# Two transformer blocks on one core: the left factors of the down products are formed beside gate and up and kept in DRAM

## The chip, the cores and the metric

One Trainium2 chip, and one of its cores. The engines of a core are TensorE (PE, the matmuls), VectorE (DVE), ScalarE (ACT), GpSimd (POOL) and SyncE (SP, which here only issues transfers). The metric is the device time of one execution in microseconds (us).

## The reference

Two transformer blocks, one behind the other, on 1024 tokens of width 1024, all in fp32. Each block ends in a feed-forward network (FFN) of hidden width 2816, and the change lies in these two:

```python
gu = jnp.einsum('bsd,df->bsf', x, w_gu)                      # block 1
gate, up = gu[..., :FFN_HIDDEN], gu[..., FFN_HIDDEN:]
ffn = jnp.einsum('bsf,fd->bsd', jax.nn.silu(gate) * up, w_down)
...
h = rmsnorm(x, g_ffn_pre[l]) * (1.0 + scale_f) + shift_f     # block 2
f = (jax.nn.silu(h @ w_gate[l]) * (h @ w_up[l])) @ w_down[l]
x = x + gate_f * rmsnorm(f, g_ffn_post[l])
```

Ahead of the first FFN stand three mixers and an output projection; ahead of the second, stick-breaking attention, a pooling mixer and another output projection. The change does not touch how these compute.

## The kernel before, in words

**Numbers.** A matmul of fp32 quality is made of three: each factor is split into a high half (a cast on ACT, line L80 or L938) and a low half (the remainder, a subtraction on DVE or POOL, L84 or L939), and `mm3` (L95 to L99) multiplies high by high, high by low and low by high.

**Gate and up** (`gate_up`, L1000 to L1058). The hidden width is 22 tiles of 128, taken as 11 pairs. The tiles of pairs 0 and 1 are multiplied directly (`direct`, tiles f = 0 to 3). Pairs 2 to 10 each go through two `Matrix` objects, `Gate` and `Up` (L899 on): seven products each, in the order 1, 6, 2, 7, 5, 4, 3, of the weights (or sums of two quarters of them, the `tt` tiles) with quarters of the activations, kept ready in SBUF as split tiles `x1B11`, `x1T2` and so on (in the second network `x3...`). `product` (L932) takes a tile `wst` from the ring of slots "w", splits the weights into it (ACT and then DVE or POOL) and issues 12 matmuls; `after` adds the sum to those of earlier products (tiles `p`, `u`, `s`). `Up.out` multiplies the silu of the gate by up (DVE for the first quarter, POOL L987 for the other three) and queues a store of the 128x512 result to `h_d` in DRAM, which ACT issues (L1056).

**Down** (`down`, L1077 on). Groups of 1, 2, 2, 2 and 2 pairs, seven products for each group. The rows of h are loaded back (`hr`) beside the weights (`wr`); sums S1 to S4 and T1 to T4 are formed (`st`), both factors are split (`hs` into slots "w", `ws` into a pool of its own). The last four tiles go directly (`down_last`, L1168) and are split there (`last`).

**What sets the order.** Each engine runs its instructions in one order, which a list scheduler writes at build time; `soon()` raises the priority of what is inside it. A tile from a ring waits for the last reader of the tile that had the slot before. The ring "w" has 6 slots and "raw" has 3. SP issues the loads, and ACT the stores of h.

Of the kernel before, what the change touches and what calls it, by code (L numbers as in the profile page):

```python
# [38 lines left out]
def two_blocks(ctx: ExitStack, tc: tile.TileContext, a):  # L39
# [657 lines left out]
    def out_proj(wo, mix_t, into, norm, put, ahead):  # L697


        mt = {0: mix_t(0)}  # L700
        for tb in range(NB + ahead):
            if tb + 1 < NB:
                mt[tb + 1] = mix_t(tb + 1)
            if tb >= ahead:
                put(tb - ahead)
            if tb < NB:
                out_block(wo, mt.pop(tb), tb, into)
                norm(tb)
# [32 lines left out]
    x1p, x1_done = pool("x1p")  # L741

    class Act:


        def __init__(self, pl, name):
            self.pl, self.name, self.t = pl, name, {}

        def half(self, th):
            if th not in self.t:  # L750
                self.t[th] = [self.pl.tile([P, KT, 512], F32R, tag="act", bufs=4, name=f"{self.name}{th}{p}")
                              for p in "hl"]
            return self.t[th]
# [25 lines left out]
    class SAct:  # L779
# [4 lines left out]
        def __init__(self, pl, name):  # L784
            self.pl, self.name, self.t = pl, name, {}

        def __call__(self, n):
            if n not in self.t:
                if n in ("T2", "T3"):

                    new = lambda nm: accp.tile([P, 4, 512], F32R, tag="acc", bufs=4, name=nm)
                else:
                    new = lambda nm: self.pl.tile([P, 4, 512], F32R, tag="act", bufs=10, name=nm)
                self.t[n] = [new(f"{self.name}{n}{p}") for p in "hl"]
            return self.t[n]
# [4 lines left out]
        def temp(self):  # L800
            return self.pl.tile([P, 4, P], F32, tag="tt", bufs=4, name="tt")
# [78 lines left out]
    x1 = SAct(x1p, "x1")  # L880
# [6 lines left out]
    out_proj(wo, lambda tb: turned(tb, 512), add1, norm1, lambda tb: x1.put(acc[tb], tb), 2)  # L887
    wo_done.close()

    x2_d = dr.tile([S, D], F32, name="x2_d")
    x3_d = dr.tile([S, D], F32, name="x3_d")
    mod_d = dr.tile([6, D], F32, name="mod_d")

    h_d = [dr.tile([P, S], F32, name=f"h_d{f}") for f in range(NFT)]
# [83 lines left out]
    class Up(Matrix):  # L981
        def out(self, i, l, t, o):
# [5 lines left out]
            self.stores.append((h_d[self.f + i][:, l * 512:(l + 1) * 512], s))  # L988

    def gate_up(act, wg, wu, nraw, npost, extra=None):  # L990

        gp, gp_done = pool("gp")
        n_raw = [0]

        def wide():
            return gp.tile([P, KT, P], F32, tag="rw", bufs=nraw, name="rw")

        def load(src):
            n_raw[0] += 1
            if nraw < 4 and n_raw[0] % 5 >= nraw:  # L1000
                r = slot("raw", [P, KT, P], F32, "raw")
            else:
                r = wide()
            DMA.dma_start(r, src)
            return r

        def post(nm):
            return gp.tile([P, 512], F32, tag="post", bufs=npost, name=nm)

        def own(tag, shape, dtype, name):  # L1010
            return gp.tile(shape, dtype, tag="rw", bufs=nraw, name=name) if tag == "w" else slot(tag, shape, dtype, name)

        def direct(f, th, g, u):
            pg = ps_lg()
            for n, (wh, wl) in enumerate((g, u)):
                for k in range(KT):
                    mm3(pg[:, n, :], wh[:, k, :], wl[:, k, :], act.at(0, k, th), act.at(1, k, th), k == 0, k == KT - 1)
            s = post("silu")
            with soon():
                A.activation(s, pg[:, 0, :], AF.Silu)  # L1020
                V.tensor_tensor(s, s, pg[:, 1, :], op=OP.mult)
            DMA.dma_start(h_d[f][:, th * 512:(th + 1) * 512], s)

        def load_gu(f, alloc=slot):
            return load_split(wg(f), [P, KT, P]), load_split(wu(f), [P, KT, P], alloc=alloc)

        wt = [load_gu(0), load_gu(1, own)]
        for th in range(2):
            for f in range(2):
                direct(f, th, *wt[f])  # L1030
        for f in (2, 3):
            wt = load_gu(f)
            for th in range(2):
                direct(f, th, *wt)
        act.sums()
        stores = []

        def flush():
            for dst, src in stores:
                A.dma_start(dst, src)  # L1040
            stores.clear()

        for p in range(2, NFT // 2):
            f = 2 * p
            ms = {}
            for m in range(2):
                w = (wg, wu)[m]
                ms[m] = (Gate, Up)[m]([load(w(f)), load(w(f + 1))], act, post)
                if m == 1:
                    ms[1].gate, ms[1].f, ms[1].stores = ms[0], f, stores  # L1050
                for q in (1, 6, 2, 7, 5, 4, 3):
                    old = list(stores)
                    stores.clear()
                    ms[m].product(q)
                    for dst, src in old:
                        A.dma_start(dst, src)  # L1056
                    if extra is not None:
                        extra(wide)  # L1058
        flush()
        gp_done.close()  # L1060

    DP = {"rw": (2 * D, 6), "st": (2 * 512, 6), "c": (2 * 512, 6), "ac": (4 * 512, 3)}

    class DownPool:


        def __init__(self, name, order):
            self.st = ExitStack()
            self.pl = {}
            for tag in order:  # L1070
                self.pl[tag], done = pool(f"{name}_{tag}")
                self.st.push(done)

        def tile(self, shape, dtype, tag, name):
            return self.pl[tag].tile(shape, dtype, tag=tag, bufs=DP[tag][1], name=name)

    def down(dp, wd, sizes, nlast, res=None):  # L1077
# [3 lines left out]
        ys = [accp.tile([P, 2, D], F32, tag="acc", bufs=4, name="acc") for _ in range(NB // 2)]  # L1081
        y = [ys[i // 2][:, i % 2, :] for i in range(NB)]
        own = {p: dp.tile([P, 4, 512], F32, "ac", f"dacc{p}") for p in (1, 6, 5)}

        def acc_of(p, c0, n):


            if p in own:
                return own[p][:, c0:c0 + n, :]
            t = ys[c0 // 2 + (0 if p in (2, 3) else 2)]  # L1090
            return t[:, c0 % 2:c0 % 2 + n, slice(0, 512) if p in (2, 4) else slice(512, D)]

        def load2(srcs, nm, small=False):
            if small:
                t = slot("raw", [P, 1, D], F32, nm)
            else:
                t = dp.tile([P, 2, D], F32, "rw", nm)
            for j, src in enumerate(srcs):
                DMA.dma_start(t[:, j, :], src)
# [601 lines left out]
```

## Time and profile before

| | us |
|---|---|
| time before, median of 3 runs | 2610.46 (2607.62 to 2612.67) |
| profiled execution, its own time | 2614.44 |
| profiled execution, its span | 2612.7 |
| PE busy | 2385.6 (91%) |
| DVE busy | 1791.0 (69%) |
| ACT busy | 1083.4 (41%) |
| POOL busy | 1031.4 (39%) |

The profiled execution lies 4.0 us above the median and has 1.7 us outside its span. By the trace, the first FFN runs from about 655 to 1400 us (direct tiles to 766, pairs from there, down from 1140, last tiles from 1340 to 1400) and the second from about 1870 to the end (pairs from 2000, down from 2360, last tiles from 2548).

### The profile page before, as it was taken

The numbers are of one execution on the slowest core, as the hardware profiler recorded it, in microseconds if no ns is written. First come the engines' busy times: TensorE is split into PE (matmuls) and PEld (weight loads), VectorE is DVE, ScalarE is ACT, GpSimd is POOL, SyncE is SP. The second block draws the span as 40 slices with busy tenths as digits, with TensorE's granted clock in tenths as the row PEclk, the third lists the DMA queues.
The fourth block names the chain that finished last, engine by engine and source line by source line (L and its number), as shares of the span: only waits on it lengthen the run. The fifth ranks groups of instructions, "written<-read, shape, count | busy, mean of one in ns | idle before, by whom it ended". The sixth has DMA issues, their size and how long they took to land.

```text
span 2612.7 us, 32305 instructions
## 1 busy us (share of the span) xinstructions
PE 2385.6 (91%) x11584; PEld 1962.2 (75%) x11584; DVE 1791.0 (69%) x2772; ACT 1083.4 (41%) x1893; POOL 1031.4 (39%) x831
## 2 busy tenths in 40 slices
PE   8888897999699999989998989889879999998997
PEld 8877776787577777867867868677657888876885
DVE  3889969646756777669976365676673555548995
ACT  4658884343223233333336334545642223225332
POOL 2520235116712222256655042435671223227646
PEclk9998998999899999989998999999989999999998
DMA  5144455423253455262304434562511222214313
GB/s 183 61 137 128 122 165 165 113 77 111 90 184 125 158 170 159 79 249 87 136 15 145 147 84 135 157 175 79 198 65 50 84 81 83 79 61 169 129 65 113
DMA packets 149787, 314.31 MB, mean 120 GB/s; under 512 B 19574, under 2 KB 65654, under 8 KB 149628
## 3 DMA queue, kind: packets, MB, share of 16 engines
q1 hardware_dynamic: 139260, 293.38, 35.4%
q10 hardware_dynamic: 10368, 18.88, 1.9%
q8 instruction: 91, 1.49, 0.2%
q14 instruction: 68, 0.56, 0.1%
HBM read 230.39 MB, written 81.81 MB: 119 GB/s over the span
## 4 chain that ended last, share of the span: by engine, by line
PE 40%; DVE 4%; POOL 3%; issue 3%; ACT 2%; DMA 2%; SPq 0%; DVEq 0%; ACTq 0%; POOLq 0%
PE plg L97 5%; PE plg L98 5%; PE plg L99 5%; PE pmm L97 5%; PE pmm L98 5%; PE pmm L99 5%; PE ptr L98 1%; PE ptr L99 1%; PE ptr L97 1%; PE plg L337 1%; POOL last L84 1%; DVE sab L1503 1%; PE ptr L1525 1%; PE pmm L692 1%; PE pmm L693 1%
## 5 line engine op out<-in xcount | busy, mean ns | idle before, releaser
L938 ACT CAST wst<-tt 128x512 fp32r<-128x512 f32 x144 | 89.3, 621 | 250.3 <-PE plg L99 202.8
L939 POOL TENSOR_TENSOR wst<-rw,wst 128x512 fp32r<-128x512 f32 x51 | 74.9, 1469 | 264.2 <-ACT wst L938 94.4
L84 POOL TENSOR_TENSOR wl<-raw,wh 128x1024 fp32r<-128x1024 f32 (+2 forms) x28 | 65.9, 2359 | 227.4 <-ACT wh L80 201.2
L337 PE MATMUL plg<-qk,qk 128*128 128x384 f32 (+4 forms) x480 | 126.1, 379 | 27.1 <-DVE mn L350 14.7
L97 PE MATMUL plg<-ws,hs 128*128 128x512 f32 x288 | 115.4, 401 | 5.2 <-DVE acc L1154 2.5
L98 PE MATMUL plg<-ws,hs 128*128 128x512 f32 x288 | 114.7, 398 | 0.0
L1503 DVE TENSOR_TENSOR_SCAN sab<-sab 128x640 f32<-128x640 f32 (+7 forms) x64 | 101.2, 1586 | 19.5 <-ACT sab L1501 18.9
L99 PE MATMUL plg<-ws,hs 128*128 128x512 f32 x288 | 114.5, 398 | 0.0
L278 ACT ACTIVATE junk_a<-xi,cand 128x1024 bf16<-128x1024 f32 (+1 forms) x124 | 109.2, 880 | 12.0 <-DVE cand L267 6.9
L337 PEld LDWEIGHTS plg<-qk,qk 128*128 128x128 f32 x480 | 82.4, 199 | 37.9 <-DVE mn L350 16.4
L939 DVE TENSOR_TENSOR wst<-tt,wst 128x512 fp32r<-128x512 f32 x144 | 105.9, 737 | 6.9 <-ACT wst L938 6.3
L84 POOL TENSOR_TENSOR hs<-hr,hs 128x1024 fp32r<-128x1024 f32 (+1 forms) x30 | 71.3, 2377 | 83.5 <-ACT hs L80 69.7
L1212 DVE SCALAR_TENSOR_TENSOR mod<-raw_c,sc,mod 128x1024 f32<-128x1024 f32 x42 | 55.9, 1331 | 57.3 <-DMA raw_c<-in_w_cond_dram 57.3
L162 PE MATMUL pmm<-wh,xh 128*128 128x256 f32 (+1 forms) x320 | 92.3, 289 | 1.6 <-DVE stgl L399 0.8
L938 ACT CAST wst<-rw 128x512 fp32r<-128x512 f32 x77 | 47.6, 619 | 108.4 <-PE plg L99 56.6
L987 POOL TENSOR_TENSOR u<-u,u 128x512 f32<-128x512 f32 x36 | 56.0, 1556 | 91.2 <-issue 43.5
L163 PE MATMUL pmm<-wl,xh 128*128 128x256 f32 (+1 forms) x320 | 91.5, 286 | 0.0
L164 PE MATMUL pmm<-wh,xl 128*128 128x256 f32 (+1 forms) x320 | 91.5, 286 | 0.0
L961 DVE TENSOR_TENSOR u<-plg,u 128x512 f32<-128x512 f32 x36 | 24.9, 690 | 96.5 <-PE plg L99 96.5
L351 ACT ACTIVATE e<-e,mn 128x128 f32<-128x128 f32 (+7 forms) x96 | 74.3, 774 | 36.1 <-DVE mn L350 35.3
L80 ACT CAST wh<-raw 128x1024 fp32r<-128x1024 f32 x54 | 56.5, 1050 | 73.2 <-PE pmm L98 30.8
L97 PE MATMUL pmm<-xh,wh 128*128 128x512 f32 x192 | 79.3, 413 | 7.4 <-DVE oB L585 4.8
(563 smaller groups left out, 8419.2 us busy)
## 6 DMA issues: line engine op xcount, KB each, us to landing
raw_c<-in_w_cond_dram SPq DMA_DIRECT2D x48, 512.0 KB, 4.1
hr<-h_d SPq DMA_DIRECT2D x44, 512.0 KB, 4.4
wr<-in_w_down_dram SPq DMA_DIRECT2D x44, 512.0 KB, 4.3
qk<-qkd SPq DMA_DIRECT2D x72, 256.0 KB, 5.7
rw<-in_wgu_dram SPq DMA_DIRECT2D x36, 512.0 KB, 4.3
x_d<-acc SPq DMA_DIRECT2D x24, 512.0 KB, 2.9
qk<-qk2d SPq DMA_DIRECT2D x48, 256.0 KB, 4.5
raw<-in_wqk_dram SPq DMA_DIRECT2D x20, 512.0 KB, 5.4
```

What stands on the lines that cost most here:

```text
L84: eng.tensor_tensor(lo, src, hi.bitcast(F32), op=OP.subtract)
L97: T.matmul(out, lh, rh, start=start, stop=False, skip_group_check=more)
L98: T.matmul(out, lh, rl, start=False, stop=False, skip_group_check=more)
L99: T.matmul(out, ll, rh, start=False, stop=stop, skip_group_check=more)
L162: T.matmul(o, at(0, k, tb * P, P), h[:, j, :], start=(k == 0), stop=False)
L163: T.matmul(o, at(0, k, tb * P, P), l[:, j, :], start=False, stop=False)
L164: T.matmul(o, at(1, k, tb * P, P), h[:, j, :], start=False, stop=(k == KT - 1))
L278: A.activation(junk_a[:, :L], xi[self.blks[i]], AF.Sign, bias=c, accum_out=self.cnt[:, i:i + 1])
L337: T.matmul(pl[:, c, :n], q[:, isl], k2[:, c * n:(c + 1) * n], start=(j == 0), stop=last)
L938: A.copy(wh, x)
L939: (G if p in (2, 4) else V).tensor_tensor(wl, x, wh.bitcast(F32), op=OP.subtract)
L1503: V.tensor_tensor_scan(sa[:, ::-1], sa[:, ::-1], sa[:, ::-1], 1.0, op0=OP.mult, op1=OP.bypass)
```

## The change

It does four things, in both networks.

- **Left factors.** After each pair, `Ffn.forms` forms what the down products will need from the left: for pairs 0 to 8 seven forms (A11, S3, S2, A22, S1, A12, S4) of 128x512, for pairs 9 and 10 the four plain quarters. `Ffn.store` splits each into high and low in a slot of the ring "w" (a tile named `hf`) and has ACT store both halves, 512 KB, to DRAM (`h_d[i][form]`, `hl_d`); the transfer of one form is issued when the next one is queued. Down loads these 512 KB per product and pair into a ring of 7 tiles that held the activations (`act.next()`), and splits only the weights, now also into slots "w" (`ws`).
- **Pools.** The pools of down (`DownPool`) are gone; weights of down come through the pool "rw" (4 tiles) and slots "raw", sums T through the pool "post", now 12 tiles. The tiles of activations have fixed places; T4 takes the place of B12.
- **First weights.** The weights of the first tile (`w0`) are loaded and split when the `Ffn` is made, which is ahead of the output projection, into the pool "rw".
- **Order at the start.** The second half of the rows is transposed and split (`late`) between the direct products of tiles 0 and 1, no longer in the output projection.

The count of PE's products is the same. Its core:

```diff
-            self.stores.append((h_d[self.f + i][:, l * 512:(l + 1) * 512], s))
...
+    class Ffn:
+        def __init__(self, act, name, g, u):
...
+            alloc = lambda tag, shape, dtype, nm: self.gp.tile(shape, dtype, tag="rw", bufs=4, name=nm)
+            self.w0 = [load_split(w, [P, KT, P], alloc=alloc) for w in (g, u)]
...
+        def flush(self):
+            for dst, src in self.stores:
+                A.dma_start(dst, src)
+            self.stores.clear()
...
+        def store(self, dst, x):
+
+            self.flush()
+            t = slot("w", [P, 2, 512], F32R, "hf")
+            split(t[:, 0], t[:, 1], x)
+            self.stores.append((dst, t.bitcast(F32)))
...
+            s1 = self.post("s1")
+            V.tensor_tensor(s1, a21, a22, op=OP.add)
+            put("A11", a11)
+            V.tensor_tensor(a21, a11, a21, op=OP.subtract)
+            put("S3", a21)
+            V.tensor_tensor(a11, s1, a11, op=OP.subtract)
+            put("S2", a11)
+            put("A22", a22)
+            put("S1", s1)
+            put("A12", a12)
+            V.tensor_tensor(a12, a12, a11, op=OP.subtract)
+            put("S4", a12)
...
+                    b[f, th] = direct(f, th, *wt[f])
+                    if th == 0:
+                        late(4 + 2 * f)
+                        late(5 + 2 * f)
+            self.forms(0, b)
...
+                self.forms(p, {(i, l): ms[0].p[i, l] for i in range(2) for l in range(2)})
+            self.flush()
...
-                hl = [slot("w", [P, 2, 512], F32R, "hs")[:, :np_, :] for _ in range(2)]
-                wl = [dp.tile([P, 2, 512], F32R, "c", "ws")[:, :np_, :] for _ in range(2)]
-                x, z = block(ln), block(rn)
-                with soon():
-                    split(*hl, x, lo_eng="pool" if p in (1, 2, 4) else "dve")
-                    split(*wl, z, lo_eng="pool" if p in (1, 3) else "dve")
...
+                    hs, ws = act.next(), []
+                    for j in range(np_):
+                        DMA.dma_start(hs.bitcast(F32)[:, 2 * j:2 * j + 2, :], h_d[f + j][ln])
+                        w = slot("w", [P, 2, 512], F32R, "ws")
+                        with soon():
+                            split(w[:, 0], w[:, 1], block(rn, j))
+                        ws.append(w)
```

**ACT where pair 2 ends and pair 3 begins, before.** The tiles `h_d_6707` and `h_d_6708` are those of pair 2, so the last store of pair 2 is in the third row from the end; a row's waits stand in brackets, by the engine or the transfers (DMAHW) that it waits for.

```order
534 L1056 DMA h_d_6708<-u_7397 128x512 [waits DMAHW5_49,Pool_49]
535 L951 COPY p_7626<-pmm 128x512 [waits DMAHW7_49,PE_49]
536 L938 CAST wst<-tt 128x512 [waits Activation_49]
537 L938 CAST wst<-rw 128x512 [waits DMAHW0_49,PE_49,Activation_49]
538 L938 CAST wst<-tt 128x512 [waits PE_49]
539 L1056 DMA h_d_6708<-p_7334 128x512 [waits DMAHW3_49,Pool_49]
540 L976 ACTIVATE s_7669<-pmm 128x512 [waits DMAHW6_49,DVE_49,PE_49]
541 L938 CAST wst<-rw 128x512 [waits DMAHW1_49,Activation_49]
542 L938 CAST wst<-tt 128x512 [waits DVE_49,PE_49,Activation_49]
543 L938 CAST wst<-rw 128x512 [waits PE_49]
544 L1056 DMA h_d_6707<-u_7356 128x512 [waits DMAHW7_49,Pool_49]
545 L938 CAST wst<-tt 128x512 [waits DVE_49,PE_49,Activation_49]
```

The same place on ACT in the changed kernel: `h_d2...` are the forms of pair 2 (6129 S3, 6130 S2, 6131 A22, 6132 S1, 6133 A12), and `wst` belongs to pair 3.

```order
561 L80 CAST hf<-u_7462 128x512 [waits DVE_49,PE_49]
562 L80 CAST hf<-s_7483 128x512 [waits DVE_49,PE_49]
563 L80 CAST hf<-u_7503 128x512 [waits DMAHW0_49,Pool_49]
564 L80 CAST hf<-s_7709 128x512 [waits PE_49]
565 L80 CAST hf<-p_7440 128x512 [waits PE_49,Pool_49]
566 L1023 DMA h_d2S_6129<-hf 128x1024 [waits DVE_49]
567 L1023 DMA h_d2S_6130<-hf 128x1024 [waits DVE_49]
568 L1023 DMA h_d2A_6131<-hf 128x1024 [waits DVE_49]
569 L1023 DMA h_d2S_6132<-hf 128x1024 [waits DMAHW4_49,DVE_49]
570 L1023 DMA h_d2A_6133<-hf 128x1024 [waits DMAHW5_49,DVE_49]
571 L80 CAST hf<-p_7440 128x512 [waits DVE_49,PE_49]
572 L945 CAST wst<-rw 128x512 [waits DMAHW1_49]
```

Before, weight casts of the next pair stand between the stores of h and wait for PE or for their data. Now five casts of forms and five stores come first, and the first weight cast of pair 3 waits for a transfer: the store of S3 (row 566), which reads the slot that this `wst` takes. The next five weight casts (rows 573 and 575 to 578) wait in the same way for the stores behind it, one each.

**PE at the same place, before.** `x1B11` is the right factor of a pair's first product, and the product with `plg<-x1B22` or `plg<-x1T1` is one of its last.

```order
3297 L97 MATMUL pmm<-x1B11h,wst 128x512 [waits Activation_49]
3298 L98 MATMUL pmm<-x1B11l,wst 128x512
3299 L1223 MATMUL pmm<-rw,ones 128x512 [waits DVE_49]
3300 L1224 MATMUL pmm<-rw,ones 128x512
3301 L97 MATMUL plg<-x1B22h,wst 128x512 [waits DVE_49]
```

And in the changed kernel:

```order
3342 L97 MATMUL plg<-x1B22h,wst 128x512
3343 L98 MATMUL plg<-x1B22l,wst 128x512
3344 L99 MATMUL plg<-x1B22h,wst 128x512
3345 L97 MATMUL pmm<-x1B11h,wst 128x512 [waits Activation_49]
3346 L98 MATMUL pmm<-x1B11l,wst 128x512
```

Before, the next pair's first product had begun ahead of the last products of this pair. Now the pair's last product is followed at once by the next pair's first, whose weights are the cast of row 572 of ACT.

**ACT at the start of the first FFN, before.** `wh` are the high halves of the first weights, `mixh` those of the output projection's left factor.

```order
468 L681 CAST mixh<-ptr 128x512 [waits PE_49,Activation_49]
469 L805 CAST x1B12h<-ptr 128x4x128 [waits DMAHW2_49,PE_49]
470 L80 CAST wh<-raw 128x1024 [waits DMAHW2_49,Activation_49]
471 L805 CAST x1B22h<-ptr 128x4x128 [waits PE_49]
472 L80 CAST wh<-raw 128x1024 [waits DMAHW5_49,DVE_49,PE_49]
473 L80 CAST wh<-raw 128x1024 [waits DMAHW0_49]
```

In the changed kernel:

```order
446 L681 CAST mixh<-ptr 128x512 [waits PE_49]
447 L80 CAST wh<-raw 128x1024 [waits DMAHW3_49,DMAHW4_49,DMAHW2_49,DMAHW0_49]
448 L80 CAST wh<-raw 128x1024 [waits DMAHW4_49,DMAHW3_49,DMAHW2_49]
449 L681 CAST mixh<-ptr 128x512 [waits PE_49]
450 L681 CAST mixh<-ptr 128x512 [waits DVE_49,PE_49]
```

The first two weight casts moved from behind the last `mixh` to ahead of the second.

## Rows read from the trace of the kernel before

**Rows 1.** The page: the span, and PE's busy time.
```profile
span 2612.7 us, 32305 instructions
PE 2385.6 (91%) x11584; PEld 1962.2 (75%) x11584; DVE 1791.0 (69%) x2772; ACT 1083.4 (41%) x1893; POOL 1031.4 (39%) x831
```
**Rows 2.** Stretches of the span: length, busy time, PE's clock, DMA share, GB/s.
```profile
core 0: us, PE busy (x) PEld busy (x) DVE busy (x) ACT busy (x) POOL busy (x), PEclk, DMA share, GB/s
...
655.00:700.00 45.00, 25.30 (x98) 19.66 (x97) 43.37 (x40) 12.66 (x19) 34.43 (x25) 0.73 0.21 80
...
760.00:1120.00 360.00, 350.83 (x1483) 279.41 (x1482) 249.93 (x316) 112.31 (x193) 99.55 (x64) 0.99 0.44 138
1120.00:1180.00 60.00, 49.15 (x170) 35.97 (x169) 44.30 (x42) 21.34 (x29) 35.62 (x18) 0.86 0.67 252
...
1330.00:1400.00 70.00, 57.00 (x245) 43.98 (x245) 47.84 (x88) 32.61 (x48) 51.10 (x66) 0.94 0.10 38
1860.00:1945.00 85.00, 60.64 (x249) 47.05 (x248) 66.05 (x85) 55.15 (x105) 57.68 (x81) 0.82 0.28 97
...
2000.00:2340.00 340.00, 337.30 (x1450) 272.44 (x1449) 189.62 (x255) 104.72 (x179) 92.01 (x61) 1.00 0.23 79
2340.00:2400.00 60.00, 47.95 (x179) 34.83 (x178) 42.20 (x29) 28.28 (x42) 38.75 (x20) 0.91 0.52 193
...
2540.00:2613.00 73.00, 56.50 (x227) 43.16 (x225) 40.73 (x52) 16.15 (x23) 40.95 (x51) 0.91 0.28 101
```
**Rows 3.** PE's waits from 655 to 700 us: total, times, longest.
```profile
PE plg L97 <- ACT wh L80: 10.4, 1, 10.4
PE ptr L815 <- DVE acc L867: 8.5, 1, 8.5
```
**Rows 4.** PE alone, a stretch inside the pairs of the second network.
```profile
2200.00:2300.00 100.00, 100.00 (x432) 1.00 0.25 85
```
**Rows 5.** Groups of instructions by shape, 2010 to 2340 us: busy, mean ns, idle before.
```profile
L987 POOL TENSOR_TENSOR u<-u,u 128x512 f32<-128x512 f32 x16 | 24.2, 1514 | 30.9 <-DMA raw<-in_wg_dram 16.5 <-DMA rw<-in_wg_dram 8.3 <-DMA hr<-h_d 4.1
L938 ACT CAST wst<-rw 128x512 fp32r<-128x512 f32 x21 | 13.0, 619 | 29.9 <-PE plg L99 19.7 <-PE ptr L99 5.0 <-PE pmm L99 2.9
L956 DVE TENSOR_TENSOR u<-ptr,p 128x512 f32<-128x512 f32 x17 | 11.6, 684 | 0.7 <-PE ptr L99 0.7
L969 DVE TENSOR_TENSOR u<-plg,u 128x512 f32<-128x512 f32 x16 | 11.1, 692 | 11.6 <-PE plg L99 11.6
```
**Rows 6.** The same view, 600 to 1130 us: splits of a 128x512 tile.
```profile
L84 DVE TENSOR_TENSOR rw<-mod,rw 128x512 fp32r<-128x512 f32 x12 | 8.2, 686 | 6.7 <-ACT rw L80 6.7
L80 ACT CAST rw<-mod 128x512 fp32r<-128x512 f32 x12 | 7.4, 619 | 11.8 <-POOL wst L939 11.8
```
**Rows 7.** ACT's queue near 2235 us, time and length of an issue.
```profile
2235.41 0.33 ACTq L1056 DMA_DIRECT2D h_d<-u  x1
```
**Rows 8.** Transfers: count, KB each, median us from issue to landing.
```profile
hr<-h_d SPq DMA_DIRECT2D x44, 512.0 KB, 4.4
wr<-in_w_down_dram SPq DMA_DIRECT2D x44, 512.0 KB, 4.3
x_d<-acc SPq DMA_DIRECT2D x24, 512.0 KB, 2.9
h_d<-u ACTq DMA_DIRECT2D x36, 256.0 KB, 2.9
h_d<-p ACTq DMA_DIRECT2D x18, 256.0 KB, 2.0
```
**Rows 9.** PE alone, 680 to 700 us: busy time, matmuls, clock.
```profile
680.00:688.00 8.00, 7.22 (x20) 0.50 0.37 131
688.00:692.00 4.00, 4.00 (x18) 0.99 0.00 0
692.00:700.00 8.00, 8.00 (x36) 1.00 0.01 2
```
**Rows 10.** Two stretches with the transfers at their fastest.
```profile
1145.00:1150.00 5.00, 4.58 (x12) 3.32 (x12) 4.96 (x6) 1.67 (x4) 3.24 (x2) 0.66 1.02 415
2365.00:2370.00 5.00, 1.79 (x5) 1.20 (x6) 5.00 (x5) 3.30 (x7) 2.91 (x2) 0.74 1.03 420
```

More of the change, by code (lines that the diff above doesn't have):

```diff
@@ L885, in norm1 @@
         DMA.dma_start(x1_d[tb * P:(tb + 1) * P, :], acc[tb])
[L887 to L897, printed above, removed]
+    NLAST, SIZES = 4, (1, 2, 2, 2, 2)
+    NPAIR = (NFT - NLAST) // 2
+    FORMS = ("A11", "S3", "S2", "A22", "S1", "A12", "S4")
+    h_d = [{n: dr.tile([P, 2, 512], F32, name=f"h_d{i}{n}") for n in FORMS} for i in range(NPAIR)]
+    hl_d = [dr.tile([P, 2, S], F32, name=f"hl_d{i}") for i in range(NLAST)]
     class Matrix:
@@ L1002, in load @@
             else:
-                r = wide()
+                r = self.gp.tile(shape, F32, tag="rw", bufs=4, name="rw")
             DMA.dma_start(r, src)
             return r
[L1007 to L1018, printed above, removed]
-            with soon():
-                A.activation(s, pg[:, 0, :], AF.Silu)
-                V.tensor_tensor(s, s, pg[:, 1, :], op=OP.mult)
-            DMA.dma_start(h_d[f][:, th * 512:(th + 1) * 512], s)
@@ L1024, in load_gu @@
[L1024 to L1032, printed above, removed]
-            for th in range(2):
[L1034 to L1058, printed above, removed]
@@ new lines, in flush, with forms @@
+        def flush(self):
[7 more added lines that the diff above has]
+            self.stores.append((dst, t.bitcast(F32)))
+        def forms(self, i, b):
+            if i >= NPAIR:
+                for (j, th), x in b.items():
+                    self.store(hl_d[2 * (i - NPAIR) + j][:, :, th * 512:(th + 1) * 512], x)
+                return
+            a11, a12, a21, a22 = b[0, 0], b[1, 0], b[0, 1], b[1, 1]
+            put = lambda n, x: self.store(h_d[i][n], x)
+            s1 = self.post("s1")
[10 more added lines that the diff above has]
+            put("S4", a12)
@@ new lines, in close, with down_last @@
+        def close(self):
+            self.tp_done.close()
+            self.act.high_done.close()
+        def down_last(self, after, between=None):
+            y, hs, ws = self.y, self.hs, self.ws
+            for tb in range(NB):
+                if tb == NB // 2 and between is not None:
+                    between()
+                ts = slice(tb * P, (tb + 1) * P)
+                for dh in range(2):
+                    dsl = slice(dh * 512, (dh + 1) * 512)
+                    o = ps_mm(512)
+                    for j in range(NLAST):
+                        mm3(o, hs[j][0][:, ts], hs[j][1][:, ts], ws[j][0][:, dsl], ws[j][1][:, dsl], j == 0, j == NLAST - 1)
+                    V.tensor_tensor(y[tb][:, dsl], y[tb][:, dsl], o, op=OP.add)
+                after(y, tb)
@@ L1192, in two_blocks @@
+    ffn1 = Ffn(x1, "f1", a["wgu"][0], a["wgu"][NFT])
+    out_proj(wo, lambda tb: turned(tb, 512), add1, norm1, lambda tb: x1.put(acc[tb], tb), 2)
+    wo_done.close()
+    ffn1.start()
+    x2_d = dr.tile([S, D], F32, name="x2_d")
+    x3_d = dr.tile([S, D], F32, name="x3_d")
+    mod_d = dr.tile([6, D], F32, name="mod_d")
     fpool, f_done = pool("fpool")
@@ L1213, in cond_steps @@
             yield
-        b = row(slot("raw", [P, D], F32, "raw_b"), a["b_cond_2"][j * D:(j + 1) * D])
+        b = slot("raw", [P, D], F32, "raw_b")
+        DMA.dma_start(b[0:1, :], a["b_cond_2"][j * D:(j + 1) * D].partition_broadcast(1))
+        V.tensor_tensor(m[0:1, :], m[0:1, :], b[0:1, :], op=OP.add)
         gn = {1: "g_mix_pre_2", 2: "g_mix_post_2", 4: "g_ffn_pre_2", 5: "g_ffn_post_2"}.get(j)
```

380 lines of the change are left out of this document (198 added, 182 removed).

## The prediction

> **What bounds the kernel now.** I read the page first: PE is busy for 2385.6 of 2612.7 us, so all other time together is 227 us [rows 1]. The stretches tell where that idle time lies. Inside the pairs there is almost none: PE works 350.8 of 360 us in the first network and 337.3 of 340 in the second [rows 2], and a stretch of 100 us there is full, with 432 matmuls at full clock, 0.231 us each [rows 4]. A product of 12 matmuls is thus 2.78 us, and a pair of 14 products 39 us. The idle time of the FFNs is at the handoffs: 19.7 us from 655 to 700, 10.9 from 1120 to 1180, 13.0 from 1330 to 1400, 24.4 from 1860 to 1945, 12.1 from 2340 to 2400 and 16.5 at the end [rows 2], 96.6 us in all. So the question has two sides: how much of these 96.6 us the change takes away, and whether it leaves the pairs as full as they are.
>
> **What the handoffs give back.** At the first start PE waits 10.4 us for a cast of the first weights and 8.5 us for the last normalized rows [rows 3]. With the weights cast earlier and the second half of the rows moved into the direct products, I take 17 of 19.7 us; at the second start, where rows and not weights are waited for, half of 24.4, 12 us. From pairs to down, half the splits go (left factors come split from DRAM), but the weights' splits remain: 9 of 10.9 and 8 of 12.1. At the last tiles only weights are split: 8 of 13.0 and 8 of 16.5. Inside down 3 us. Sum 65 us, two thirds of what there is. The bounds: 30 if only the waits of [rows 3] and half of the second start's go, since the early casts themselves stand on ACT ahead of casts of the output projection and wait for four transfers; 100 if all goes.
>
> **What the boundaries between pairs cost.** This term decides. Before, the next pair's first product begins ahead of the last products of its predecessor, and a stall would need its weights late; their casts wait for PE alone. In the changed order the last product of a pair is followed directly by the first of the next, and that one waits for an ACT cast into a slot of "w" that still holds S3's halves. The slot is free when the store of S3 has landed. S3 is A11 less A21, and A21 hangs on the pair's last product. So PE stands from the end of the last product until this chain is through:
> - DVE adds the last product to `u`, 0.69 us (L969), and POOL multiplies by the silu, 1.51 us (L987) [rows 5];
> - DVE forms S1 and S3, not in the trace; the nearest are other 128x512 sums of two tiles at 0.68 to 0.69 us [rows 5]: 1.38 us;
> - ACT casts five forms, 5 x 0.62 = 3.10 us [rows 6], before it comes to the store of S3; the low half of S3 (DVE, 0.69 us [rows 6]) lies beside them;
> - ACT issues the store, 0.33 us [rows 7];
> - the store of 512 KB lands. The nearest row is another store of 512 KB, `x_d<-acc`, at 2.9 us; bounds are 2.0 (a 256 KB store on ACT's queue) and 4.4 (a 512 KB load) [rows 8];
> - ACT casts the weights, 0.62 us [rows 5].
>
> The sum is 10.5 us. Nothing hides it: PE's row has no other product in between. After tiles 0 and 1, and after 2 and 3, there is no POOL multiplication, so 9.0 us there. Each network has 7 boundaries of the first kind (pairs 2 to 8 into the next) and 2 of the second: 14 x 10.5 + 4 x 9.0 = 183 us. Pair 9 has no sums, and its stores gate only later slots; there four casts stand before the weights: 0.69 + 1.51 + 4 x 0.62 + 0.62 = 5.3 us, twice, 11 us. What follows pair 10 is counted in the handoffs.
>
> The landing is the part on which the skill has a rule. The Trainium skill, page "DMA: Bandwidth & Descriptors", section "Anatomy of one DMA — SWDGE (gpsimd) path", says that a transfer's semaphore fires only when its last byte is confirmed in the target memory, slowest with HBM, and gives about 2.0 us plus bytes over 436 GB/s for a path that is not the one used here. By that a store of 512 KB would be 3.2 us, an estimate from that page, against the 2.9 us of the row, and the sum over 18 boundaries would be 5 us larger. It speaks against reusing a slot right behind a store.
>
> **The clock.** After the wait at 664 PE resumed at half clock: from 680 to 688 us it did 20 matmuls at a granted clock of 0.50, where 692 to 700 has 36 at 1.00 [rows 9]. Sixteen matmuls of 0.22 us are 3.5 us. A shorter wait also left a dip: the stretch from 2365 us has a clock of 0.74 [rows 10]. I take 3.5 us for each of the 18 boundaries, 63 us; bounds are 0 (no fall) and 7 (twice as long at the half).
>
> **What costs nothing, and why.** Seven splits of low halves and three sums per pair add about 10 x 0.69 = 7 us to DVE in 39 us; DVE is busy 250 of 360 us in the first network's pairs and 190 of 340 in the second's [rows 2], so it has the room, and should it not, the price is at most these 7 us per pair, 126 us. Seven casts of 0.62 on ACT (112 of 360 us busy) have even more. Loads in down replace sums and splits; they are hidden as long as they come at their rate (a rival below). Removed splits in down save no time inside it, where PE is nearly full.
>
> **Sum.** 183 + 11 + 63 - 65 = 192 us more. On the profiled execution's 2614.4 us this is 2806 us. That execution lies 4.0 us above the median of before, which is small beside the terms. Low end: landing 2.0 us, so 14 x 9.6 + 4 x 8.1 = 167, plus 11, no clock lost, 100 gained: 2692. High end: landing 4.4 us, so 14 x 12.0 + 4 x 10.5 = 210, plus 11, plus 18 x 7 = 126, 30 gained: 2931.
>
> **Rivals.**
> - **Boundaries are nearly free (faster).** If the next pair's first weights were cast before the forms take the ring, or the stores released their slots while PE still had products, only the handoffs would count: 2614 - 65 = 2549 us. It decides the sign at 65/18 = 3.6 us per boundary, clock included. For it: transfers are far from their limit in the pairs (DMA share 0.44 and 0.23 [rows 2]). Against it: the casts alone are 3.1 us, and they come after a DVE and a POOL step that PE's last product releases. Chance 0.06. The Trainium skill, page "Trainium Kernel Development and Optimization", section "Best Practices", advises to double-buffer so that DMA overlaps with compute; by that rule a ring of six slots should hide the stores. In the order of this change it does not, since seven forms fill six slots.
> - **Stores at the pace of the transfers.** The next six weight tiles wait for six stores, 3.1 MB beside the weights' loads. At the 138 GB/s of the first network's pairs [rows 2] they take 22.8 us, against 16.7 us of six products: 6 us more at 18 boundaries, 2916 us. Against it: 415 GB/s at a share of 1.02 [rows 10] show that 138 is what was asked for, not a limit. Chance 0.12.
> - **Down waits for its loads.** 63 forms of 512 KB, four of 1 MB and 22 weight tiles are 49 MB per network. At 252 GB/s (1120 to 1180 us [rows 2]) that is 193 us and hidden; at 138 GB/s 353 us, some 100 more than down takes now, so 3006 us. Chance 0.07.
> - **Gains and costs meet**, within 0.2%, which is about what a measurement of this kernel can tell from no change: 0.02.
>
> **How the numbers follow.** The likeliest case, slower by the boundaries' chain, has 0.73 and gives 2806 us; its own range is 2692 to 2931. The second rival lies inside this range, the first and third and the exact tie outside, 0.15 together, so the range given is 2700 to 2935. Faster is the first rival, 0.06; same 0.02; slower the rest, 0.92.
>
> **What would show it.** In the changed profile PE has idle times of 9 to 12 us, nine per network and some 39 us plus that apart, put down to an ACT cast `wst` whose own wait is for a transfer `hf`; the 14 between pairs are longer than the 4 at the direct tiles. PE's clock dips behind each. The gate and up stretches grow from 360 and 340 us by about 120 each, while the handoffs shrink. The mean landing of the stores is near 2.9 us. I am wrong if these idle times are below 4 us, if the clock stays at 1.00 behind them (then near 2743 us), if PE's waits in down are for loads of `h_d`, or if the handoffs keep their 97 us (then near 2871 us).

## The result and the profile after

The change made the kernel slower: 2849.9 us (median of 4 runs) against 2609.0 us, a ratio of 1.0925 with a 95% interval of 1.0903 to 1.0947. The forecast was 2806 us in a range of 2700 to 2935.

The page of the changed kernel, its span, busy times and transfers:

```profile
span 2852.0 us, 33007 instructions
PE 2413.8 (85%) x11584; PEld 1982.8 (70%) x11584; DVE 1848.8 (65%) x3042; ACT 1104.1 (39%) x2013; POOL 780.3 (27%) x751
q10 hardware_dynamic: 22496, 74.46, 6.6%
HBM read 278.65 MB, written 133.19 MB: 144 GB/s over the span
```

PE has as many matmuls as in [rows 1] and is a little longer busy with them (28 us); the span grew by 239 us. So 211 us of it are time in which PE waits. What PE waited for, over the whole span (total, times, longest, in us):

```profile
PE pmm L97 <- ACT wst L945: 184.3, 18, 13.0
PE plg L97 <- DVE p L971: 26.0, 30, 4.7
PE plg L97 <- ACT wh L80: 22.0, 2, 11.9
PE plg L97 <- DVE u L968: 15.7, 15, 2.6
PE plg L337 <- DVE mn L350: 12.9, 7, 4.2
PE ptr L826 <- DVE x1B12l L817: 11.0, 2, 7.8
```

The first row is the boundary between pairs: 18 waits, nine in each network, for the first weights of the next pair. The third is the same at the direct tiles, once in each network. The second and fourth grew as well, and the prediction did not have them. The rows of before that answer to the first, second and fourth:

```profile
PE pmm L97 <- ACT wst L938: 1.2, 3, 0.5
PE plg L97 <- DVE p L964: 3.4, 4, 1.2
PE plg L97 <- DVE u L961: 4.7, 5, 1.8
```

The stages, from the first and last matmul of each in the traces, show where the 239 us lie. `own_two` is an experiment of the next section.

| stage (us) | before | changed | difference | own_two |
|---|---|---|---|---|
| output projection and direct tiles, 1 | 290.8 | 298.0 | +7.2 | 279.0 |
| pairs, 1 | 374.9 | 503.5 | +128.6 | 410.3 |
| down, 1 | 196.6 | 179.2 | -17.4 | 170.5 |
| last tiles, projections, attention | 385.9 | 384.3 | -1.6 | 382.4 |
| output projection and direct tiles, 2 | 276.4 | 288.6 | +12.2 | 276.4 |
| pairs, 2 | 357.2 | 489.3 | +132.1 | 363.8 |
| down, 2 | 192.9 | 180.0 | -12.9 | 167.6 |
| last tiles, 2 | 64.6 | 55.6 | -9.0 | 55.6 |

The stretches of the changed kernel that answer to [rows 2], pairs and down of each network (columns as there):

```profile
771.00:1230.00 459.00, 343.73 (x1366) 268.20 (x1364) 307.97 (x395) 133.19 (x231) 88.13 (x59) 0.89 0.43 150
1290.00:1440.00 150.00, 150.00 (x657) 123.07 (x656) 118.10 (x161) 37.23 (x60) 9.21 (x6) 1.00 0.68 244
2127.00:2572.00 445.00, 338.12 (x1345) 262.84 (x1344) 239.05 (x327) 127.23 (x221) 83.27 (x59) 0.90 0.28 104
2630.00:2780.00 150.00, 150.00 (x656) 123.09 (x657) 110.71 (x147) 45.33 (x75) 7.74 (x6) 1.00 0.67 242
```

Pairs that kept PE full before leave it idle for a quarter of their time, at a mean clock of 0.89. Down is the other way round: 150 of 150 us busy at 242 to 244 GB/s. No row of PE's waits there names a load of forms.

One boundary, that between pairs 3 and 4 of the second network, on ACT. The last product of pair 3 ended on PE at 2239.9 us:

```profile
2243.71 0.62 ACT L80 CAST hf<-u 128x512 fp32r<-128x512 f32 x1 [12.90 <-DVE u L1044]
2244.43 0.62 ACT L80 CAST hf<-s 128x512 fp32r<-128x512 f32 x1
2244.96 0.61 ACT L80 CAST hf<-u 128x512 fp32r<-128x512 f32 x1
2245.08 0.33 ACTq L1023 DMA_DIRECT2D h_d3S<-hf  x1
2245.48 0.61 ACT L80 CAST hf<-s 128x512 fp32r<-128x512 f32 x1
2245.81 0.33 ACTq L1023 DMA_DIRECT2D h_d3S<-hf  x1
2246.00 0.61 ACT L80 CAST hf<-p 128x512 fp32r<-128x512 f32 x1
2246.41 0.33 ACTq L1023 DMA_DIRECT2D h_d3A<-hf  x1
2247.01 0.97 ACTq L1023 DMA_DIRECT2D h_d3S<-hf  x1
2248.07 1.15 ACTq L1023 DMA_DIRECT2D h_d3A<-hf  x1
2249.32 0.62 ACT L80 CAST hf<-p 128x512 fp32r<-128x512 f32 x1 [2.71 <-issue]
2249.84 0.61 ACT L945 CAST wst<-rw 128x512 fp32r<-128x512 f32 x1
```

And on PE, its first matmuls after the wait:

```profile
2250.51 0.80 PE L97 MATMUL pmm<-x3B11h,wst 128*128 128x512 f32 x1 [10.48 <-ACT wst L945]
2251.11 0.63 PE L98 MATMUL pmm<-x3B11l,wst 128*128 128x512 f32 x1
```

PE stood for 10.48 us, and then each matmul took 0.63 us where 0.39 to 0.40 is usual. This is the chain of the prediction, with one link changed. ACT reaches the weight cast 0.52 us after the cast of S4's form, with no wait of its own. The store of S3, issued at 2245.08, had landed by then: the trace has the last update of its semaphore at 2247.72 us, 2.64 us after the issue and 2.1 us before the weight cast. At all 14 boundaries between pairs this landing took 2.62 to 2.68 us, and the weight cast follows 0.52 to 0.53 us behind S4's. What ended last is ACT's own row: five casts, five store issues, of which the fourth waited 0.3 us for its low half on DVE and the fourth and fifth took 0.97 and 1.15 us, and the cast of S4.

### The profile page after: what moved, and what is told of

Read it like the earlier page. It is cut to its first block, busy times and chain, and to the rows that moved or that the text cites. A ratio compares the mean times of both kernels' runs of the same rounds, so it can differ in the third digit from the quotient of the medians.

```text
span 2852.0 us, 33007 instructions
## 1 busy us (share of the span) xinstructions
PE 2413.8 (85%) x11584; PEld 1982.8 (70%) x11584; DVE 1848.8 (65%) x3042; ACT 1104.1 (39%) x2013; POOL 780.3 (27%) x751
## 5 line engine op out<-in xcount | busy, mean ns | idle before, releaser
L946 POOL TENSOR_TENSOR wst<-rw,wst 128x512 fp32r<-128x512 f32 x57 | 83.7, 1468 | 384.8 <-ACT wst L945 363.3
L337 PE MATMUL plg<-qk,qk 128*128 128x384 f32 (+4 forms) x480 | 124.7, 377 | 27.9 <-DVE mn L350 12.9
L97 PE MATMUL pmm<-x1B11h,wst 128*128 128x512 f32 x72 | 35.0, 486 | 93.4 <-ACT wst L945 93.4
L97 PE MATMUL pmm<-x3B11h,wst 128*128 128x512 f32 x72 | 36.3, 504 | 90.9 <-ACT wst L945 90.9
L80 ACT CAST hf<-u 128x512 fp32r<-128x512 f32 x36 | 22.1, 615 | 189.7 <-DVE u L1044 150.2
L80 ACT CAST ws<-st 128x512 fp32r<-128x512 f32 x72 | 45.0, 628 | 123.6 <-PE plg L99 77.1
L1171 DVE TENSOR_TENSOR dacc<-dacc,plg 128x1024 f32<-128x1024 f32 x48 | 58.6, 1220 | 52.6 <-PE plg L99 52.6
L97 PEld LDWEIGHTS pmm<-x1B11h,wst 128*128 128x128 f32 x72 | 16.8, 233 | 101.2 <-ACT wst L945 97.3
L97 PEld LDWEIGHTS pmm<-x3B11h,wst 128*128 128x128 f32 x72 | 17.4, 241 | 98.8 <-ACT wst L945 94.8
L692 PE MATMUL pmm<-woh,mixh 128*128 128x512 f32 x192 | 79.0, 411 | 4.8 <-ACT mixh L681 2.7
```

The costliest lines, as they stand in the source:

```text
L80: A.copy(hi, src)
L97: T.matmul(out, lh, rh, start=start, stop=False, skip_group_check=more)
L337: T.matmul(pl[:, c, :n], q[:, isl], k2[:, c * n:(c + 1) * n], start=(j == 0), stop=last)
L692: T.matmul(o, mh[:, k, :], wh[:, dsl], start=(k == 0), stop=False)
L946: (G if p in (2, 4) else V).tensor_tensor(wl, x, wh.bitcast(F32), op=OP.subtract)
```

## Experiments

**Own slots for the forms.** Theory: PE stops because seven forms take all six slots of the weights' ring and stand ahead of the weights in ACT's row. Rival: the added casts, sums and stores cost by themselves.

```diff
-            t = slot("w", [P, 2, 512], F32R, "hf")
+            t = self.pp.tile([P, 2, 512], F32R, tag="hf", bufs=2, name="hf")
...
-            return self.pp.tile([P, 512], F32, tag="post", bufs=12, name=nm)
+            return self.pp.tile([P, 512], F32, tag="post", bufs=8, name=nm)
```

> The forms get two slots of their own instead of slots of the weight ring "w" (the space comes from the pool "post", 8 tiles instead of 12). All casts, sums and stores are still done. Theory: what stops PE is that the next pair's first weights stand behind the forms, in the ring (their slots are held until stores land) and in ACT's row. Then the 16 idle times of 10.5 to 13 us at the pairs' boundaries go, and with them the half clock behind them and the two waits of 0.88 us in each pair: 15.7 us per pair, about 250 us in all, so near 2600 us (2580 to 2640). Rival 1, the added casts, sums and 74 MB of stores cost by themselves: stays above 2780 us. Rival 2, stores come too slowly: idle times of PE move into the pair, since two slots let only two stores be under way, 2680 us or more.

Measured: 2577.6 us, ratio to before 0.9868 (0.9853 to 0.9884). That is 272 us less than the change and 1.3% faster than the kernel before. PE's waits for weights in the pairs, over the whole span:

```profile
PE pmm L97 <- ACT wst L945: 3.0, 4, 0.8
PE ptr L97 <- ACT wst L945: 1.9, 4, 0.7
```

184 us have become 5; 8 more are waits for the weights' low halves on DVE. The work, the stores and their bytes are those of the change, so the rival is refuted. The forms wait for landings still: on ACT, between 2100 and 2140 us of this run, these rows stand:

```profile
ACT hf L80 <- DVE u L1044: 2.0, 1, 2.0
ACT hf L80 <- DMA h_d4A<-hf: 0.9, 1, 0.9
ACT hf L80 <- DMA h_d4S<-hf: 0.9, 1, 0.9
```

The scheduler now sets weights of the next pair between the forms, and from 1990 to 2340 us PE waits for 2.8 us in all.

**A single slot of their own.** As before, with `bufs=1` for `hf` and 10 tiles of `post`.

> As own_two, but with a single slot for the forms ("post" has 10 tiles), so each form's cast waits until the store before it has landed: 0.62 + 0.69 + 0.33 + about 3.5 us, 5.1 us a form, 36 us for seven in a pair of 39 us. Theory: as this still fits into a pair, the time is that of own_two within 15 us. Rival 2, stores' pace: 30 us or more above own_two. Rival 1: above 2780 us.

Measured: 2585.7 us, ratio 0.9898 (0.9879 to 0.9918), 8 us above own_two. Seven stores, one behind the other, still fit beside a pair. The rival of stores at the pace of the transfers is refuted for the kernel's own traffic.

**The forms spread over the next gate, in the shared ring.** `forms` becomes a generator, and one step is taken after each product.

```diff
                     for q in (1, 6, 2, 7, 5, 4, 3):
                         ms[m].product(q)
+                        next(left, None)
...
```

> The forms share the ring "w" as in the change, but one form is queued after each product of the next pair's gate instead of seven in a row at the boundary. Each weight tile then waits for a store that was issued some three products (8 us) earlier. Theory: a store lands about 3.5 us after its issue, so nearly all of the 250 us comes back: 2590 to 2650 us. Rival 1 (added work by itself): above 2780 us. Rival 3 (any sharing of the ring with stores costs, wherever it is): each of seven waits leaves a gap of about 1 us and more, 2700 us or above.

Measured: 2795.2 us, ratio 1.0698 (1.0675 to 1.0721). The theory's number was wrong here, and that of rival 3 was right: the burst is only part of it. PE's waits, whole span:

```profile
PE pmm L97 <- ACT wst L945: 101.2, 20, 10.5
PE plg L97 <- ACT hf L80: 24.3, 9, 3.3
PE plg L97 <- DVE p L971: 21.1, 18, 3.4
```

A form in the ring holds a slot from its cast until its store has landed, so the six slots no longer reach six products ahead (this last is argued from the code). They are not rival 3's seven small waits: in the second network most pairs have one of 5.3 us for a weight and another of 2.1 to 3.3.

**Plain forms first.** A11, A22 and A12 come first, then S3, S2, S1, S4.

```diff
+            put("A11", a11)
+            put("A22", a22)
+            put("A12", a12)
             s1 = self.post("s1")
...
-            put("A11", a11)
...
-            put("A22", a22)
             put("S1", s1)
-            put("A12", a12)
```

> Only the order of the seven forms is changed: A11, A22 and A12, which do not hang on the pair's last product, come first, and then S3, S2, S1, S4. The first two weight tiles of the next pair then take slots of A22 and A12, whose stores land early; the third takes that of S3. In ACT's row the first weight cast still stands behind the casts of S3, S2 and S1 and one of S4. Theory of the landing (the store of S3 ends last): the idle time of 10.5 us shrinks by the landing and issue, about 3 us, so 16 x 3 + some clock, 2780 to 2810 us. Rival (ACT's row of casts, store issues and casts ends last; in the trace S3's store seems to have landed before ACT comes to the weights): the idle time shrinks by what leaves ACT's row ahead of the first weight cast, four store issues of 0.33 to 1.15 us, also about 3 us, but the time between the cast of S4 and the weight cast stays 0.5 us in both, with no wait for a transfer.

Measured: 2791.9 us, ratio 1.0691 (1.0673 to 1.071); the idle time at a boundary is 6.8 us. Both theories had the size. What tells them apart is ACT's row. By the trace's semaphores the store of A22, issued at 2244.5 us, landed at 2247.1, and that of A12, issued at 2248.5, at 2251.1; still the first weight's cast comes only at 2254.9, 0.52 us behind the cast of S4 (which slot it takes, these rows don't show):

```profile
2253.78 0.33 ACTq L1023 DMA_DIRECT2D h_d4S<-hf  x1
2254.39 0.62 ACT L80 CAST hf<-p 128x512 fp32r<-128x512 f32 x1
2254.91 0.61 ACT L945 CAST wst<-raw 128x512 fp32r<-128x512 f32 x1
```

**Two of the stores on SP.** Does the landing of S3's store or ACT's row of issues end the chain in the change?

```diff
-                A.dma_start(dst, src)
+                eng.dma_start(dst, src)
...
-        def store(self, dst, x):
+        def store(self, dst, x, eng=A):
...
-            put = lambda n, x: self.store(h_d[i][n], x)
+            put = lambda n, x: self.store(h_d[i][n], x, DMA if n in ("S1", "A12") else A)
```

> The change as it is, but two of the five stores that stand ahead of the next pair's first weights in ACT's row (those of S1 and A12, whose issues took 0.97 and 1.15 us there) are issued by SP instead. The store of S3, on which the first weight's slot hangs, stays first and stays on ACT. If the landing of that store ends the chain: idle times stay at 10.5 us and the time at 2850 us within 8. If ACT's row of issues ends it: the cast of S4 and the weights come 1 to 1.3 us earlier, idle times of 9.2 to 9.5 us, and the time falls by 16 to 21 us, near 2830 us. SP may delay the weights' loads behind these stores, which would add.

Measured: 2838.7 us, ratio 1.0877 (1.0846 to 1.0909), 11 us less than the change; the idle times between pairs are 9.55 us instead of 10.5. By the theory of the landing they would have stayed at 10.5. It is ACT's row, and with the issues gone the next link shows, S4's sum on DVE:

```profile
2239.06 0.62 ACT L80 CAST hf<-p 128x512 fp32r<-128x512 f32 x1 [1.78 <-DVE p L1051]
2239.59 0.61 ACT L945 CAST wst<-rw 128x512 fp32r<-128x512 f32 x1
```

The gain was under the 16 us expected: all these waits together fell by 11 us, from 184.3 to 173.3, since one of them in the first network grew to 14.6.

**Seven and eight slots in a shared ring.** Weights and forms share the six slots of "w" and one or two more from a pool, to which every fourth tile goes (with seven slots, every seventh). The edit for eight:

```diff
+        def wslot(self, shape, name):
+            self.nw += 1
+            if self.nw % 4 == 0:
+                return self.pp.tile(shape, F32R, tag="wx", bufs=2, name=name)
+            return slot("w", shape, F32R, name)
```

> The change with a ring of eight slots that weights and forms still share: six of "w" and two from a pool, taken strictly in turn, so every slot comes round after eight uses. It has the space of own_two ("post" 8 tiles, two slots more), and only the assignment differs: in own_two the two slots hold nothing but forms. Theory: the next pair's first weights now take a slot of an earlier weight and the second those of A11, only the third wait for S3's store; two products (5.6 us) cover part of the 10.5 us. Idle of about 5 us in all at a boundary, 16 x (5.6 + up to 3 of clock and waits), 2700 to 2760 us. Rival (any two slots more would do): near own_two, 2578 us. Rival (the ring does not matter): 2850 us.

> The same with seven slots in turn ("post" has 10 tiles, one slot more). Theory: the first weight takes A11's slot, whose store has long landed, and the second waits for S3's store: one product (2.8 us) of cover, 16 x 2.8 plus some clock, 2785 to 2810 us, about halfway between the change (2850) and shared8. Rivals as there.

Measured: 2794.3 us with eight (ratio 1.07, 1.0684 to 1.0716) and 2797.8 us with seven (1.0711, 1.0692 to 1.0731). PE's waits for weights, whole span, eight slots first:

```profile
PE pmm L97 <- ACT wst L945: 68.4, 12, 11.6
PE ptr L97 <- ACT wst L945: 59.5, 10, 8.2
```

```profile
PE pmm L97 <- ACT wst L945: 136.5, 18, 10.9
```

Seven came out at the expected time, but not in the expected way: PE still waits for the first weight, 7.1 us at most boundaries, whose cast at one of them (2205.68 us) stands behind five casts of forms and ahead of the last two issues and S4's cast. Eight did not: one more slot brought 3.5 us where some 60 were expected. PE waits there for the first weight at some boundaries and for the second at others, and at the four looked at (2154 to 2303 us) the cast that it waits for stands in ACT's row behind one to six casts of the forms. The slots are not taken in turn, as the expectation had it: the first weight of pair 7 was cast at 2346.65 us, while PE read the last weight of pair 6 until 2349.2, so it had another slot than that one. Why the scheduler sets the casts so was not traced. With the same space as own_two this is 217 us slower, so it is what shares the slots that counts and not their number.

**Own slots, early weights undone.**

```diff
-            self.w0 = [load_split(w, [P, KT, P], alloc=alloc) for w in (g, u)]
+            self.w0 = lambda: [load_split(w, [P, KT, P], alloc=alloc) for w in (g, u)]
...
-            wt = [self.w0, load_gu(1)]
+            wt = [self.w0(), load_gu(1)]
```

> own_two (2577.6 us) with the early weights undone: the first tile's weights are loaded and cast at the start of gate and up, not ahead of the output projection. The prediction gave the early weights about 10 us of its 17 at the first start and little at the second; by own_two's stages the first start got 12 us shorter and the second nothing. If the early weights are what shortened it: 10 to 14 us slower than own_two, near 2589 us. If it was the move of the second half of the rows into the direct products: within 5 us of own_two.

Measured: 2590.6 us, ratio 0.9927 (0.9904 to 0.995), 13 us above own_two; in the profiled executions the two starts are 3.9 and 4.2 us longer. The early weights are worth about 8 to 13 us in all. The time is the one expected if they had shortened the first start by its 12 us, but by luck: only 3.9 us of it lie there. What gave the other 8 was not tried apart.

**Own slots, low halves on POOL.**

```diff
-            split(t[:, 0], t[:, 1], x)
+            split(t[:, 0], t[:, 1], x, lo_eng="pool")
```

> own_two with the low halves of the forms formed by POOL instead of DVE. In own_two the pairs of the first network still take 35 us more than before (410 against 375), in the second 6, and DVE is busy 325 of 390 us in the first (246 of 350 in the second). If that remainder is DVE's load: the 7 x 0.69 us of nine pairs leave DVE, and 15 to 30 us come back in the first network, 2550 to 2565 us. If it is the transfers (201 against 158 GB/s) or the order: within 8 us of own_two, or slower, since POOL takes about 1.4 us for each and shares its work with the weights' low halves.

Measured: 2588.7 us, ratio 0.9918 (0.9894 to 0.9942), 11 us above own_two. The move did not relieve DVE. From 750 to 1140 us, own_two first and this run second (columns as in [rows 2]):

```profile
750.00:1140.00 390.00, 364.12 (x1495) 283.11 (x1494) 325.18 (x421) 144.16 (x249) 108.95 (x63) 0.98 0.57 201
```

```profile
750.00:1140.00 390.00, 360.40 (x1477) 279.13 (x1476) 325.04 (x358) 143.28 (x247) 193.97 (x121) 0.98 0.55 193
```

DVE has 63 instructions fewer and is busy for the same 325 us. Its other work took longer, the low halves of weights for one, in the same two runs:

```profile
L946 DVE TENSOR_TENSOR wst<-tt,wst 128x512 fp32r<-128x512 f32 x72 | 53.2, 741 | 10.7 <-ACT wst L945 10.6
```

```profile
L946 DVE TENSOR_TENSOR wst<-tt,wst 128x512 fp32r<-128x512 f32 x72 | 71.4, 995 | 15.3 <-ACT wst L945 15.3
```

The Trainium skill, page "GPSIMD Engine Reference", section "1. Specifications", has it that GpSimd shares its SBUF interfaces with VectorE and contends with instructions there that have two SBUF inputs. This row is such an instruction, and 741 ns becoming 995 while POOL's busy time rose from 109 to 194 us agrees with it. So does L963, which reads one of its inputs from PSUM (`ptr`) and stayed at 682 and 681 ns. L1252, with two SBUF inputs, did not slow (1527 and 1487 ns), so two SBUF inputs alone do not tell which rows pay.

**Own slots, forms spread.**

> The forms have two slots of their own as in own_two, and are queued one after each product of the next pair's gate as in spread (2795 us). If the loss in spread came from sharing the ring alone: within 15 us of own_two, 2565 to 2595 us. If spreading the forms itself costs (they hold tiles of "post" for longer, 8 of them): well above 2600 us.

Measured: 2635.6 us, ratio 1.0091 (1.0063 to 1.0119), 58 us above own_two, so spreading costs something even without the shared ring. PE waits for a sum on DVE in most pairs of the first network, up to 8.0 us:

```profile
PE plg L97 <- DVE u L966: 27.6, 7, 8.0
```

A spread form holds tiles of `post` for most of the next gate, and there are 8 here; that this is what the sum waits for was not tried. So of the 218 us by which `spread` lies above own_two, some 58 come with the spreading itself, and not with the ring.

**Own slots, every store twice.**

```diff
                 A.dma_start(dst, src)
+                A.dma_start(h2_d[next(n_h2)], src)
```

> own_two (2577.6 us) with every store of a form issued a second time, to a place in DRAM that nothing reads: 74 MB more written and seven more issues per pair on ACT. By the theory the stores cost nothing once no weight waits for them: in 39 us a pair would write 7.3 MB beside some 4 MB of loads, 290 GB/s, below the 415 GB/s seen in before; within 20 us of own_two. Rival (the pace of stores is near its limit, which would make own_two's remaining loss in the first network's pairs one of transfers): 40 us or more above own_two.

Measured: 2615.6 us, ratio 1.0016 (1.0001 to 1.0032), 38 us above own_two, between the two expectations. Doubled, the traffic is no longer free (271 GB/s in the first network's pairs, a DMA share of 0.75). What it costs undoubled was not measured apart.

**Own slots, less work on DVE.** All but the first of eight products of each conditioning row are left out of the first network's pairs; their loads stay.

```diff
             if k == 0:
                 V.tensor_scalar_mul(m, r, sc[:, 0:1])
-            else:
-                V.scalar_tensor_tensor(m, r, sc[:, k:k + 1], m, op0=OP.mult, op1=OP.add)
             yield
```

> own_two with work left out of DVE in the first network's pairs: the second block's conditioning rows, which are summed there from eight products each, keep only the first product (42 multiply-adds of 1.5 us are left out, 64 us of DVE; their loads stay). The output's conditioning is therefore that of one eighth of the rows. If DVE's load is what makes own_two's pairs of the first network 35 us longer than before's (410 against 375 us): 20 to 35 us come back there, 2540 to 2558 us, with the second network unchanged. If it is the stores' traffic (own_twice, with that doubled, was 38 us slower than own_two): within 8 us of own_two, 2570 to 2586 us.

Measured: 2562.5 us, ratio 0.982 (0.9781 to 0.986), 15 us under own_two and 4 above the upper end of what was expected; the pairs of the first network went from 410.3 to 390.3 us and those of the second stayed. The four executions lie between 2554.9 and 2574.4 us, and the stages are from one execution of each. So with 64 us of work less on DVE some 20 of the 35 us come back by which own_two's pairs there are longer than before's; the work left out is not the work that the change added, so this shows that DVE's load counts there and not what the forms cost. The other 15 are open.

## Why the prediction was right, and where it was off

**Boundaries.** The step that decided held: the last product of a pair is followed by a wait for the first weights of the next. The prediction had 10.5 us for it; 12 of the 14 waits between pairs are 10.47 to 10.51 us, two are 11.3 and 12.2, and pair 9's are 4.4 (5.3 predicted). Behind tiles 2 and 3 it was 13.0 instead of 9.0. In sum PE's first row above is 184 us, where these terms were 176.

**The last link of the chain was wrong, though the sum was right.** The prediction put 0.33 us of issue and 2.9 us of landing behind the casts. In the trace the landing is over before it is needed; some_sp and plain_first show that ACT's own row ends last, four more store issues and S4's cast, 3.2 us by chance. The landing itself took 2.64 us, where the prediction took 2.9. The rule on completion of the Trainium skill, page "DMA: Bandwidth & Descriptors", section "Anatomy of one DMA — SWDGE (gpsimd) path", weighed in the prediction, therefore did not set the time of the boundary, and the 3.2 us estimated there for another path are longer than the 2.64. That the forms in the weights' ring are the cause of the whole, own_two shows. Whether they act by slots held until a store lands, or by the place in ACT's row that the weights get behind them, was not separated; at the boundaries measured the price is paid on ACT.

**Signs that went otherwise.** The first weight cast waits for no transfer, as said. The waits at the direct tiles (10.1 to 13.0 us) are not the shorter ones: their chain has the silu on ACT, 0.60 us, which the prediction left out, and behind tiles 2 and 3 DVE also forms sums of weights (L925) between its steps, 1.58 and 1.15 us near 2130 us.

**A missed term.** With no weights of the next pair at hand, the pair's last three products follow each other without another between them, and each of the last two waits until DVE has read the product just before it: 0.88 us twice in most pairs. The rows L971 and L968 grew to 41.7 us from 8.1 us before (L964 and L961), 34 us. In own_two, where products of two pairs mix again, the row of L968 is gone and this is left:

```profile
PE plg L97 <- DVE p L971: 11.4, 5, 3.5
```

The order at the boundary that the prediction quoted shows this cover going; the prediction priced it for the first product alone.

**The clock.** 3.5 us per boundary were predicted. In a stretch of 55 us of the changed kernel, one pair, PE is busy for 42.3 us at a clock of 0.91, where 39 were needed [rows 4]: 3.3 us. The row has length, PE's busy time, clock, DMA share and GB/s:

```profile
2240.00:2295.00 55.00, 42.33 (x169) 0.91 0.29 105
```

**Handoffs.** The prediction gave the starts 17 and 12 us. They brought 11.8 and nothing (own_two's stages, which have no boundary there): the second half of the rows, moved into the direct products, is waited for there instead, in the changed kernel 11.0 us in the first network (`x1B12l`). This is the largest of the wrong terms in proportion. The other handoffs and down were to bring 36 us and brought 41. That most of the handoffs' idle time would go was right for the places where splits went away, and wrong where rows are waited for.

**Work put at nothing.** The prediction gave DVE room for the added splits and sums. Where the boundaries are gone, in own_two, the pairs of the first network still take 35 us more than before, and DVE, there busy for 250 of 360 us before [rows 2], is busy for 325 of 390; own_less_dve shows that its load counts. How much of this the change itself pays was not measured.

**Sum.** Pairs 261 us against 232 predicted, starts with the boundary behind tiles 0 and 1 19 against -4, down and last tiles -41 against -36: 239 against 192. Within the pairs, the waits for weights (184 us), the missed term (34) and the clock (16 times 3.3 us, 53) make 271 us; what gave 10 back was not looked for.

**The rivals.** The faster one was nearer than its chance told: with the forms in slots of their own the boundaries do cost little, and the kernel takes 2578 us where 2549 was the rival's number. It fails in the change itself by the shared ring alone. Stores at the pace of the transfers, and down waiting for loads, did not occur. The number of the latter was too small as it stood: 353 us are some 155 to 160 more than the 197 and 193 us that down took before, not 100, which makes about 3120 us and not 3006.

## What to carry to other kernels

A slot that a store reads is busy until the store has landed, and a ring that works as a lookahead for the bottleneck engine loses that lookahead when such tiles take turns in it: give outgoing tiles slots of their own, even one or two, before adding slots to a shared ring. Read the row of the bottleneck engine at the boundary in the new order: if its last step of one unit is followed at once by the first of the next, the whole chain between them is exposed, and small waits that other work used to cover come back too. And when a chain's sum agrees with the trace, check its links one by one; here a landing and a row of issues had the same length.

## What the runs showed that was not expected

A burst of 512 KB stores on ACT goes with slower issues: in one boundary the first three took 0.33 us each, the fourth 0.97 and the fifth 1.15, at every boundary of the second network within 0.02 us; in own_two the 14 between 2100 and 2200 us, which come one or two at a time, took 0.33. And moving 63 subtractions from DVE to POOL left DVE as busy as it was, 325 of 390 us, because its remaining work slowed down by nearly as much.
